# Norm weights on the rows of the output projections' weights, nine working tiles on 2 KB places, and the scores of two token tiles in one run

## The chip, the cores and the metric

The kernel runs on one core of a Trainium2 chip. Its engines work side by side, each through its own list of instructions in order: TensorE (PE) multiplies matrices into PSUM (eight banks of 128 partitions x 512 fp32 values), VectorE (DVE) and ScalarE (ACT) work on PSUM and SBUF, GpSimd (POOL) on SBUF only, and SyncE (SP) issues most of the transfers. An instruction that needs another engine's result waits for a semaphore, and everything behind it on its engine waits too. The metric is device time in microseconds, the median of several runs.

## The reference

Two layers of a trunk on a sequence of 512 tokens and a model width of 1024, all in fp32. Each layer normalises its input, projects it to 7,696 columns, runs four mixers on parts of these columns (retention, differential attention, a state-space mixer called SSD, and an mLSTM), each 512 wide, and adds the output projection of the four results:

```python
for l in range(DEPTH):
    u = rmsnorm(h, norm_w[l])
    ret_p, diff_p, ssd_p, ml_p = split_cols(u @ w_in[l], ...)
    ret_out  = retention_mixer(...) * silu(rz)
    diff_out = diff_attention_mixer(...) * silu(dz)   # _rms(out) * norm_w * (1.0 - lam_init)
    ssd_out  = _rms(y * silu(sz)) * ssd_norm_w[l]
    ml_out   = mlstm_mixer(...) * silu(mz)            # _layernorm(h) * norm_w
    mix = concatenate([ret_out, diff_out, ssd_out, ml_out])
    h = h + mix @ w_out[l]
return rmsnorm(h, final_norm_w)
```

Three of the mixers end in a norm with a weight for each of its columns; retention's has none. The differential attention has four heads with two sets of 64-wide queries and keys each: `s = q k` for both sets, a causal softmax of each, and `a = p0 - lam * p1` is multiplied with the values.

## The kernel before

**Tiles.** Tokens stand in four tiles of 128. The normalised input lies transposed in `uh` and `ul` (a rounded fp32r part and the rest), and each weight block of 128 x 512 is split the same way: `split_half` (L322) makes `whi` by a copy on ACT and `wlo` by a subtraction on DVE. A product is then three fp32r matmuls (hi-hi, lo-hi, hi-lo). `load_block` (L337) fetches a 512-column block of the input weights, `out_proj` (L552) the output weights of one mixer: four row blocks of 128 for each half of the 1024 columns, so eight split halves a mixer and layer.

**Order.** PE's order is written out by the program while it is built. `ORDER` (L48) lists the projections; they are the filler. The mixers are generators that the planner (`later`, `spawn`, `drive`, L120 to 147) interleaves with the filler: it adds up an estimated PE time (`clk`), and a mixer that yields a number is continued when that much estimated time has gone by. The numbers are in `W` (L55). `psum` (L169) hands out the eight PSUM banks, always the one that is planned to be free first; `free` gives a bank back with a `lag`, the estimated time until its readers are done. If the real readers are later, PE waits. The order of DVE, ACT, POOL and SP is chosen by the framework's scheduler, from the priorities of the instructions and its own costs (except in the start, where it is written out).

**The differential attention** (`diff`, L1031). For each head it splits the queries (`qs`), waits `dQ`, and then goes through the token tiles 0, 1, 2, 3. Tile t has (t+1) x 128 keys. Two banks take the scores of the two sets, by six matmuls of 64 rows each, two at a time on the two halves of the array (L1051). For each set DVE adds the mask on the diagonal block (L1055) and takes the negative maximum (L1056), ACT takes the exponential with its row sum (L1057); then DVE combines the two (L1061 to 1064). `diff_av` (L1071) comes `dT` + t x `dT1` later: it transposes `a` on PE, copies it out on ACT (odd tiles, L1078) or DVE (even tiles, L1080), and `dV` later multiplies it with the values into one bank for the head. Between the tiles lie waits of `dN` + t x `dN1` (1, 2, 3 and 4 in estimated us). `diff_fin` normalises the head and multiplies by `z` on POOL.

**Norm weights.** `ev_silu` (L459) evacuates the gate projections: tanh on ACT, `z` on DVE (L467). For `mz` and `dz` POOL then multiplies `z` by the row of the mixer's norm weights, broadcast over the partitions (L1154, L1158). For the SSD the weights come in at the end of `fin_s` (L936, on DVE). The broadcast rows lie in `rows`, 4,736 bytes a partition.

**The mLSTM** (`mlstm`, L744). For each token tile DVE builds a weight matrix by four instructions of 128 columns (L762), ACT takes its exponential (L764), DVE multiplies the scores by it (L769) and PE goes on with the result. POOL meanwhile scales queries (L758), and `fin_m` multiplies an earlier tile by `z` (L838).

**Places.** All tiles but the constants and `h` come from one pool. Working tiles `w` of 2 KB a partition are used in turn, seven of them; a score tile's two exponentials take one each.

## Time and profile before

| | us |
|---|---|
| median of 3 runs | 1041.19 |
| lowest and highest | 1039.27 and 1041.24 |
| profiled execution, its own time | 1043.25 |
| its span in the profile | 1041.2 |
| PE busy in the span | 1021.6 |
| DVE busy | 703.6 |
| ACT busy | 471.8 |
| POOL busy | 193.2 |

The span is the time between the first and the last instruction of the program; what lies around it (2.05 us in that execution) belongs to the execution's time. Matmuls are pipelined, so a busy PE is not necessarily a PE at its peak: the distance between the starts of two matmuls tells how fast it goes. Rows of the timeline hold start, duration, engine, line, operation, what is written and read, and how many instructions were merged; rows of groups hold the sum and the mean, and then the idle time before them and what ended it.

### The profile page before, as it was taken

Reading aid. Unit: us, or ns where it says so; the run is one execution under the profiler, and the core shown is the slowest. Engines: PE = TensorE matmul, PEld = TensorE weight load, DVE = VectorE, ACT = ScalarE, POOL = GpSimd, SP = SyncE. Lnnn points to the kernel's source line nnn. Section 1 sums busy time; section 2 is a strip of 40 time slices with the busy share of each in tenths; the row PEclk is TensorE's granted clock in tenths of the full one; section 3 lists DMA queues with packets and bytes.
Section 4 is the critical chain, followed back from the end, with each engine's and each line's share of the span. In section 5 each row is a group of like instructions: output and inputs, shape, how many; then the busy total and the mean of one; then the engine's idle time right before and its main releaser. Section 6 shows DMA issues by size and latency. Waiting matters only on the chain.

```text
span 1041.2 us, 14256 instructions
## 1 busy us (share of the span) xinstructions
PE 1021.6 (98%) x5116; PEld 834.7 (80%) x5116; DVE 703.6 (68%) x1501; ACT 471.8 (45%) x1050; POOL 193.2 (19%) x221
## 2 busy tenths in 40 slices
PE   7999999999999999999999999999999999999997
PEld 5788888877778888878887888787777888888786
DVE  5587686567777868546555967666577887773454
ACT  4444336644445444423353543575444553543322
POOL 3000143102111144022000013420021112520301
PEclk9999999999999999999999999999999999999999
DMA  7324322322212423323122432323132224233112
GB/s 296 108 73 120 102 71 82 101 82 82 60 42 88 132 64 101 115 71 126 42 82 82 129 94 72 91 81 102 62 97 65 82 82 122 82 95 108 49 54 82
DMA packets 39143, 95.54 MB, mean 92 GB/s; under 512 B 3592, under 2 KB 16520, under 8 KB 38944
## 3 DMA queue, kind: packets, MB, share of 16 engines
q1 hardware_dynamic: 38064, 93.18, 29.2%
q10 hardware_dynamic: 1008, 1.44, 0.4%
q8 instruction: 40, 0.66, 0.3%
q14 instruction: 31, 0.25, 0.1%
HBM read 92.47 MB, written 2.15 MB: 91 GB/s over the span
## 4 chain that ended last, share of the span: by engine, by line
PE 95%; DVE 3%; DMA 1%; ACT 1%; issue 0%; POOL 0%; SPq 0%; POOLq 0%; DVEq 0%; ACTq 0%
PE pspj L114 79%; PE psacc L114 6%; PE psS L114 6%; PE psS L118 4%; DVE wlo L329 1%; DMA cst<-in_consts_dram 1%; DVE w L762 1%; DVE z L467 0%; DVE s L1056 0%; ACT e L230 0%; ACT whi L327 0%; DVE e L305 0%; DVE z L1221 0%; DVE w L769 0%; DVE h L580 0%
## 5 line engine op out<-in xcount | busy, mean ns | idle before, releaser
L329 DVE TENSOR_TENSOR wlo<-raw,whi 128x512 fp32r<-128x512 f32 x298 | 212.0, 730 | 61.9 <-ACT whi L327 55.8
L327 ACT CAST whi<-raw 128x512 fp32r<-128x512 f32 x300 | 179.7, 619 | 129.4 <-PE pspj L114 77.4
L114 PE MATMUL pspj<-whi,uh 128*128 128x512 f32 x512 | 209.2, 409 | 0.9 <-DVE whi L327 0.6
L114 PE MATMUL pspj<-whi,ul 128*128 128x512 f32 x512 | 200.5, 392 | 0.0
L114 PE MATMUL pspj<-wlo,uh 128*128 128x512 f32 x512 | 199.9, 391 | 0.0
L114 PE MATMUL pspj<-uh,whi 128*128 128x512 f32 x448 | 179.1, 400 | 0.0
L114 PE MATMUL pspj<-uh,wlo 128*128 128x512 f32 x448 | 174.9, 390 | 0.0
L114 PE MATMUL pspj<-ul,whi 128*128 128x512 f32 x448 | 174.6, 390 | 0.0
L114 PEld LDWEIGHTS pspj<-whi,uh 128*128 128x128 f32 x512 | 96.6, 189 | 23.8 <-issue 3.0
L114 PEld LDWEIGHTS pspj<-wlo,uh 128*128 128x128 f32 x512 | 96.1, 188 | 21.0
L114 PEld LDWEIGHTS pspj<-whi,ul 128*128 128x128 f32 x512 | 96.8, 189 | 17.6 <-DVE ul L316 0.2
L114 PE MATMUL pspj<-whi,mh 128*128 128x512 f32 (+1 forms) x260 | 106.3, 409 | 3.6 <-DVE w L1080 3.6
L114 PE MATMUL pspj<-whi,ml 128*128 128x512 f32 (+1 forms) x260 | 103.1, 397 | 0.0
L114 PE MATMUL pspj<-wlo,mh 128*128 128x512 f32 (+1 forms) x260 | 102.9, 396 | 0.0
L114 PEld LDWEIGHTS pspj<-uh,wlo 128*128 128x128 f32 x448 | 84.1, 188 | 18.2
L114 PEld LDWEIGHTS pspj<-uh,whi 128*128 128x128 f32 x448 | 84.2, 188 | 17.3 <-issue 0.7
L114 PEld LDWEIGHTS pspj<-ul,whi 128*128 128x128 f32 x448 | 84.3, 188 | 15.9
L217 POOL TENSOR_TENSOR s<-s,nhalf 128x4 f32<-128x4 f32 (+1 forms) x44 | 36.1, 819 | 320.4 <-DVE s L1104 130.5
L509 DVE SCALAR_TENSOR_TENSOR e<-pspj,cvh,e 128x511 f32<-128x511 f32 (+2 forms) x90 | 66.9, 744 | 9.8 <-ACT e L507 8.7
L527 ACT ACTIVATE e<-pspj 32x512 f32<-32x512 f32 x96 | 56.6, 590 | 19.6 <-PE pspj L114 18.3
L580 DVE TENSOR_TENSOR h<-pspj,h 128x512 f32<-128x512 f32 (+1 forms) x65 | 43.6, 678 | 30.7 <-PE pspj L114 30.2
L114 PEld LDWEIGHTS pspj<-whi,mh 128*128 128x128 f32 x260 | 49.6, 191 | 15.3 <-DVE w L1080 4.4
(215 smaller groups left out, 1361.7 us busy)
## 6 DMA issues: line engine op xcount, KB each, us to landing
raw<-in_w_in_dram SPq DMA_DIRECT2D x118, 512.0 KB, 3.9
raw<-in_w_out_dram SPq DMA_DIRECT2D x32, 512.0 KB, 3.5
bcm<-adr SPq DMA_DIRECT2D x16, 256.0 KB, 3.4
bcm<-gdr SPq DMA_DIRECT2D x8, 256.0 KB, 3.4
out_dram<-z SPq DMA_DIRECT2D x7, 256.0 KB, 2.0
h<-in_x_dram SPq DMA_DIRECT2D x3, 512.0 KB, 8.4
rows<-in_rows_dram SPq DMA_DIRECT2D x2, 592.0 KB, 9.0
cst<-in_consts_dram SPq DMA_DIRECT2D x1, 1035.0 KB
```

What stands on the lines that cost most here:

```text
L114: self.nc.tensor.matmul(out, lhsT=lhsT, rhs=rhs, start=start, stop=stop, **kw)
L118: self.nc.tensor.transpose(out, src, self.ident if ident is None else ident)
L217: self.nc.gpsimd.tensor_tensor(out=out, in0=m, in1=self.nhalf[:, :n], op=ALU.pow)
L327: (nc.vector.tensor_copy if vector else nc.scalar.copy)(out=hi, in_=raw)
L329: eng.tensor_tensor(out=lo, in0=raw, in1=hi.bitcast(F32), op=ALU.subtract)
L509: nc.vector.scalar_tensor_tensor(acc[:, s:], p[:, 0:S - s], w[:, 3 - s:4 - s], acc[:, s:], ALU.mult, ALU.add)
L527: nc.scalar.activation(x[q * 32:q * 32 + 32, :], p[o * 32:o * 32 + 32, :], AF.Copy, scale=scale)
L580: nc.vector.tensor_tensor(out=hs, in0=p, in1=hs, op=ALU.add)
L762: nc.vector.scalar_tensor_tensor(w[:, h * P:(h + 1) * P], gb[:, h, :], self.al[:, t, h:h + 1], self.cap, ALU.add, ALU.min)
```

## The change

**Norm weights.** The weights of the three norms are no longer rows but columns: they stand behind the convolution parameters in `cv` (`V_M`, `V_S`, `V_D`), one column of 128 for each row block of the output weights. When `out_proj` splits the weights of these three mixers, each row is multiplied by its norm weight: ACT's copy becomes a scaled copy and DVE's subtraction a scaled subtraction. The POOL products at L1154 and L1158 are gone, and the end of `fin_s` becomes a scaled copy on ACT. Retention's weights are split as before. `rows` shrinks to 128 bytes a partition.

**Tiles and places.** Nine working tiles instead of seven (the lines that only say so are left out below, as is the removal of the two POOL products). The one pool becomes several: small tiles first, then `h` and the tiles of 2 KB and multiples of it, then the parameter columns, so that each large tile begins at a multiple of 2 KB.

**Scores.** For each head the token tiles go in two pairs, (2, 0) and (3, 1). The twelve score matmuls of a pair follow each other. Tile 0's scores lie in the last quarter of tile 2's banks; tiles 3 and 1 have two banks each. All banks of a pair are freed together with a lag of 4.0. Tiles 0 and 1 hold both exponentials in one working tile. `diff_av` of the first tile of a pair comes `dT` (now 9.0) later, that of the second another 3.0; the wait behind a pair is 5.0.

```diff
@@ -41,20 +41,28 @@
 GROUPS = {"r": 0, "d": 1, "s": 2, "m": 3}
-R_DNW, R_SNW, R_MNW, R_GB, R_AL, R_SD, R_LAM = 0, 128, 640, 1152, 1168, 1176, 1184
-R_W = 1184
+R_GB, R_AL, R_SD, R_LAM = 0, 16, 24, 32
+R_W = 32
+V_M, V_S, V_D, V_W = 80, 84, 88, 89
 ORDER = ["mv", "gates", "mq", "mk", "mlstm", "mo", "mz", "dk", "dq", "diff", "dv", "dz", "m", "xs", "bc", "ssd", "d",
          "rqk", "sz", "rv", "ret", "rz", "s", "r"]
+BIG = {"w", "e", "whi", "wlo", "uh", "ul", "bcm", "raw", "z", "ft", "mh", "ml", "qs"}
+END = {"cv", "cvh", "nlam", "aneg"}
 QS = 4
 W = {'norm': 9.0, 'g1': 1.5, 'g2': 7.3, 'g3': 1.8, 'g4': 12.4, 'mB': 1.8, 'mB3': 3.0, 'mC': 1.3, 'mN': 5.0, 'mF': 9.6, 'sB': 10.2,
-     'sN': 0.0, 'sF': 7.3, 'rC': 2.3, 'rN': 3.0, 'dT': 9.14, 'dN': 1.0, 'dM': 3.0, 'dV': 6.68, 'dF': 14.0,
-     'm0': 6.4, 's0': 8.8, 'dT1': 0.6, 'dN1': 1.0, 'hp': 100, 'he': 100, 'hr': 50, 'hd': 50, 'dS': 4.7, 'dQ': 6.0,
+     'sN': 0.0, 'sF': 7.3, 'rC': 2.3, 'rN': 3.0, 'dT': 9.0, 'dN': 5.0, 'dM': 3.0, 'dV': 6.68, 'dF': 14.0,
+     'm0': 6.4, 's0': 8.8, 'dT1': 3.0, 'hp': 100, 'he': 100, 'hr': 50, 'hd': 50, 'dS': 4.7, 'dQ': 6.0,
      'ha': 50}
...
@@ -96,7 +104,12 @@
         self.dbg = dbg or {}
         mk = lambda n, b, **k: ctx.enter_context(tc.tile_pool(name=n, bufs=b, **k))
         self.cp = mk("cp", 1)
+        self.small = mk("small", 1)
+        self.hp = mk("hp", 1)
         self.pool = mk("pool", 1)
+        self.end = mk("end", 1)
         self.ps = mk("ps", 1, space=bass.MemoryType.PSUM)
         self.banks = [(0.0, b) for b in range(8)]
         self.bank = {}
...
@@ -153,10 +166,11 @@
     def t(self, tag, shape, dt=F32, bufs=None):
         self.n += 1
-        return self.pool.tile(shape, dt, tag=tag, name=f"{tag}_{self.n}", bufs=bufs)
+        pool = self.pool if tag in BIG else self.end if tag in END else self.small
+        return pool.tile(shape, dt, tag=tag, name=f"{tag}_{self.n}", bufs=bufs)
     def pg(self):
-        return self.t("w", [P, 512], bufs=7)
+        return self.t("w", [P, 512], bufs=9)
     def ev(self):
         return self.t("e", [P, 512], bufs=4)
...
@@ -269,12 +283,14 @@
         nc = self.nc
         rows, lam, cv = self.prm
         self.cvh = self.t("cvh", [P, 2, 8, 5], bufs=2)
-        nc.vector.tensor_scalar(self.cvh, cv, 0.5, None, ALU.mult)
+        nc.vector.tensor_scalar(self.cvh, cv[:, 0:V_M].rearrange("p (a b c) -> p a b c", a=2, b=8), 0.5, None, ALU.mult)
         self.rw = lambda o, w: rows[:, o:o + w]
         lam_init = 0.8 - 0.6 * math.exp(-0.3 * l)
-        self.dnw = self.rw(R_DNW, P)
-        nc.vector.tensor_scalar(self.dnw, self.dnw, 0.5 * (1.0 - lam_init), None, ALU.mult)
-        lp = self.t("w", [P, 2, 64], bufs=7)
+        nc.vector.tensor_scalar(cv[:, V_D:V_W], cv[:, V_D:V_W], 0.5 * (1.0 - lam_init), None, ALU.mult)
+        self.nwc = {"m": [cv[:, V_M + k:V_M + k + 1] for k in range(4)],
+                    "s": [cv[:, V_S + k:V_S + k + 1] for k in range(4)],
+                    "d": [cv[:, V_D:V_W]] * 4, "r": [None] * 4}
+        lp = self.t("w", [P, 2, 64], bufs=9)
         ld = lam.rearrange("p (a b c) -> p a b c", a=2, b=2)
         nc.vector.tensor_tensor(out=lp, in0=ld[:, :, 0, :], in1=ld[:, :, 1, :], op=ALU.mult)
         ls = self.sm([P, 2])
...
@@ -319,24 +335,28 @@
                 yield 0
         self.done.add(("u", l, t))
-    def split_half(self, raw, j, vector=False):
+    def split_half(self, raw, j, vector=False, scale=None):
         nc = self.nc
         hi = self.t("whi", [P, 512], F32R, bufs=10)
         lo = self.t("wlo", [P, 512], F32R, bufs=10)
         with self.tc.high_priority(W["hp"]):
-            (nc.vector.tensor_copy if vector else nc.scalar.copy)(out=hi, in_=raw)
-            eng = nc.vector if j else nc.gpsimd
-            eng.tensor_tensor(out=lo, in0=raw, in1=hi.bitcast(F32), op=ALU.subtract)
+            if scale is not None:
+                nc.scalar.activation(hi, raw, AF.Copy, scale=scale)
+                nc.vector.scalar_tensor_tensor(lo, raw, scale, hi.bitcast(F32), ALU.mult, ALU.subtract)
+            else:
+                (nc.vector.tensor_copy if vector else nc.scalar.copy)(out=hi, in_=raw)
+                eng = nc.vector if j else nc.gpsimd
+                eng.tensor_tensor(out=lo, in0=raw, in1=hi.bitcast(F32), op=ALU.subtract)
         return hi, lo
-    def split_w(self, src, g):
+    def split_w(self, src, scales=(None, None)):
         raw = self.t("raw", [P, 2, 512], bufs=2)
         self.nc.sync.dma_start(out=raw, in_=src)
-        return [self.split_half(raw[:, j, :], 1) for j in range(2)]
+        return [self.split_half(raw[:, j, :], 1, scale=scales[j]) for j in range(2)]
     def load_block(self, name):
         b = BIDX[name]
-        return [q for g in range(4) for q in self.split_w(self.win[self.l, b, :, 2 * g:2 * g + 2, :], g)]
+        return [q for g in range(4) for q in self.split_w(self.win[self.l, b, :, 2 * g:2 * g + 2, :])]
     def start(self, evac):
...
@@ -552,7 +570,9 @@
     def out_proj(self, g, mixt, tok_outer=False, after=None, cut=False, heads=False):
         nc = self.nc
         gi = GROUPS[g]
-        w = [[x for q in range(2) for x in self.split_w(self.wout[self.l, gi, half, :, 2 * q:2 * q + 2, :], 2 * half + q)]
+        nw = self.nwc[g]
+        w = [[x for q in range(2) for x in self.split_w(self.wout[self.l, gi, half, :, 2 * q:2 * q + 2, :],
+                                                        nw[2 * q:2 * q + 2])]
              for half in range(2)]
         l = self.l
         order = [(t, hf) for t in range(NT) for hf in range(2)] if tok_outer else \
...
@@ -933,7 +953,7 @@
         self.rsqrt(f, m, 1)
         mix = self.pg()
         nc.vector.tensor_scalar(f, f, 0.5, None, ALU.mult)
-        nc.vector.scalar_tensor_tensor(mix, yd, f, self.rw(R_SNW, 512), ALU.mult, ALU.mult)
+        nc.scalar.activation(mix, yd, AF.Copy, scale=f)
         yield W["sF"]
         self.emit(l, t, "s", mix, res)
...
@@ -1038,33 +1058,44 @@
             o = self.psum("acc")
             r = self.sm([P, NT, 2], tag="rsum")
             ca = self.sm([P, NT])
-            for t in range(NT):
-                n = (t + 1) * P
-                ts_ = slice(t * P, n)
-                nm = self.sm([P, 2])
-                pe = [self.pg(), self.pg()]
-                sj = [self.psum("S"), self.psum("S")]
-                for i, (a, b) in enumerate(((0, 0), (0, 1), (1, 0))):
-                    for j, s in enumerate(sj):
-                        own = slice(j * 64, j * 64 + 64)
-                        self.mm(s[:, 0:n], lhsT=qp[a][own, ts_], rhs=k[h][b][own, 0:n], start=(i == 0), stop=(i == 2),
-                                share=0.5)
-                with self.tc.high_priority(W["hd"]):
-                    for j, s in enumerate(sj):
-                        nc.vector.tensor_tensor(out=s[:, ts_], in0=s[:, ts_], in1=self.mlow, op=ALU.add)
-                        nc.vector.tensor_reduce(out=nm[:, j:j + 1], in_=s[:, 0:n], axis=AX.X, op=ALU.max, negate=True)
-                        nc.scalar.activation(pe[j][:, 0:n], s[:, 0:n], AF.Exp, bias=nm[:, j:j + 1],
-                                             accum_out=r[:, t, j:j + 1])
-                        self.free(s, lag=2.5)
-                    rr = self.sm([P, 1])
-                    nc.vector.reciprocal(out=rr, in_=r[:, t, 1:2])
-                    nc.vector.scalar_tensor_tensor(ca[:, t:t + 1], rr, r[:, t, 0:1], self.nlam, ALU.mult, ALU.mult)
-                    a = pe[0]
-                    nc.vector.scalar_tensor_tensor(a[:, 0:n], pe[1][:, 0:n], ca[:, t:t + 1], pe[0][:, 0:n],
-                                                   ALU.mult, ALU.add)
-                self.spawn(self.diff_av(l, t, h, a, o, v), W["dT"] + t * W["dT1"])
-                yield W["dN"] + t * W["dN1"]
+            for tt in ((2, 0), (3, 1)):
+                bank = [self.psum("S"), self.psum("S")]
+                sj = {}
+                for i, t in enumerate(tt):
+                    n = (t + 1) * P
+                    if i and tt[0] == 2:
+                        sj[t] = [b[:, 3 * P:4 * P] for b in bank]
+                    else:
+                        if i:
+                            bank += [self.psum("S"), self.psum("S")]
+                        sj[t] = [b[:, 0:n] for b in bank[-2:]]
+                    new = not i or tt[0] == 3
+                    for m, (a, b) in enumerate(((0, 0), (0, 1), (1, 0))):
+                        for j, s in enumerate(sj[t]):
+                            own = slice(j * 64, j * 64 + 64)
+                            self.mm(s, lhsT=qp[a][own, t * P:n], rhs=k[h][b][own, 0:n], start=(new and m == 0),
+                                    stop=(m == 2), share=0.5, skip_group_check=True)
+                for i, t in enumerate(tt):
+                    n = (t + 1) * P
+                    nm = self.sm([P, 2])
+                    p0 = self.pg()
+                    pe = [p0[:, 0:n], p0[:, n:2 * n] if t < 2 else self.pg()[:, 0:n]]
+                    with self.tc.high_priority(W["hd"]):
+                        for j, s in enumerate(sj[t]):
+                            sd = s[:, t * P:n]
+                            nc.vector.tensor_tensor(out=sd, in0=sd, in1=self.mlow, op=ALU.add)
+                            nc.vector.tensor_reduce(out=nm[:, j:j + 1], in_=s, axis=AX.X, op=ALU.max, negate=True)
+                            nc.scalar.activation(pe[j], s, AF.Exp, bias=nm[:, j:j + 1], accum_out=r[:, t, j:j + 1])
+                        rr = self.sm([P, 1])
+                        nc.vector.reciprocal(out=rr, in_=r[:, t, 1:2])
+                        nc.vector.scalar_tensor_tensor(ca[:, t:t + 1], rr, r[:, t, 0:1], self.nlam, ALU.mult, ALU.mult)
+                        a = pe[0]
+                        nc.vector.scalar_tensor_tensor(a, pe[1], ca[:, t:t + 1], a, ALU.mult, ALU.add)
+                    self.spawn(self.diff_av(l, t, h, a, o, v), W["dT"] + i * W["dT1"])
+                self.free(*bank, lag=4.0)
+                yield W["dN"]
             self.spawn(self.diff_fin(h, o, r, zs, res, l))
             yield W["dM"]
...
@@ -1253,11 +1277,13 @@
     wo = i["w_out"].reshape(DEPTH, 4, 4, P, 2, 512)
     wo = np.ascontiguousarray(wo.transpose(0, 1, 4, 3, 2, 5))
     nrm = np.concatenate([i["norm_w"], i["final_norm_w"][None]], 0)
-    rows = np.concatenate([i["diff_norm_w"], i["ssd_norm_w"], i["mlstm_norm_w"], i["ssd_dt_bias"], i["mlstm_gate_b"],
-                           i["ssd_a_log"], i["ssd_d"], i["diff_lambda"].reshape(DEPTH, -1)], 1)
+    rows = np.concatenate([i["ssd_dt_bias"], i["mlstm_gate_b"], i["ssd_a_log"], i["ssd_d"],
+                           i["diff_lambda"].reshape(DEPTH, -1)], 1)
     cv = [np.concatenate([i[n + "_w"], i[n + "_b"][:, None]], 1).reshape(DEPTH, 5, 8, P)
           for n in ("ssd_conv", "mlstm_conv")]
-    cv = np.ascontiguousarray(np.stack(cv, 1).transpose(0, 4, 1, 3, 2))
+    cv = np.stack(cv, 1).transpose(0, 4, 1, 3, 2).reshape(DEPTH, P, -1)
+    cols = [i[n].reshape(DEPTH, -1, P).transpose(0, 2, 1) for n in ("mlstm_norm_w", "ssd_norm_w", "diff_norm_w")]
+    cv = np.ascontiguousarray(np.concatenate([cv] + cols, 2))
     return {"x": np.ascontiguousarray(i["x"][0]), "w_in": wb, "w_gate": wg, "w_out": wo,
             "norms": np.ascontiguousarray(nrm), "rows": np.ascontiguousarray(rows), "conv": cv, "consts": _consts()}
```

More of the change, by code (lines that the diff above doesn't have):

```diff
@@ L186, in setup @@
         nc = self.nc
-        self.h = [self.cp.tile([P, D], F32, name=f"h{t}") for t in range(NT)]
+        self.h = [self.hp.tile([P, D], F32, name=f"h{t}") for t in range(NT)]
         for half in range(2):
@@ L456, in proj_feat, with ev_silu @@
                 self.free(p, lag=3.0)
-    def ev_silu(self, dst, tag, bufs, nwt=None):
+    def ev_silu(self, dst, tag, bufs):
         nc = self.nc
@@ L467, in f @@
             nc.vector.scalar_tensor_tensor(z, th, 1.0, p, ALU.add, ALU.mult)
-            if nwt is not None:
-                nwt(z)
             dst.append(z)
@@ L606, in gates @@
             yield 0
-        gf = self.t("w", [32, 512], bufs=7)
+        gf = self.t("w", [32, 512], bufs=9)
         nc.scalar.copy(out=gf, in_=p[0:32, :])
@@ L665, in gates @@
         nc.vector.tensor_scalar(self.ncs, cs[:, :, 0:8], -1.0, None, ALU.mult)
-        st = self.t("w", [P, NT, 96], bufs=7)
+        st = self.t("w", [P, NT, 96], bufs=9)
         nc.gpsimd.memset(st, 0.0)
@@ L677, in gates @@
             self.tr(pr[0:96, t * P:(t + 1) * P], st[:, t, :])
-        arow = self.t("w", [8, 512], bufs=7)
+        arow = self.t("w", [8, 512], bufs=9)
         nc.scalar.copy(out=arow, in_=pr[0:8, :])
@@ L681, in gates @@
         nc.sync.dma_start(out=self.adr, in_=arow)
-        alr = self.t("w", [4, 512], bufs=7)
+        alr = self.t("w", [4, 512], bufs=9)
         nc.scalar.copy(out=alr, in_=pr[32:36, :])
@@ L686, in gates @@
         self.free(pr)
-        mr = self.t("w", [96, 512], bufs=7)
+        mr = self.t("w", [96, 512], bufs=9)
         nc.gpsimd.memset(mr, 0.0)
@@ L1151, in mixer @@
             return f
-        def times_mnw(z):
-            nc.gpsimd.tensor_tensor(out=z, in0=z, in1=self.rw(R_MNW, 512), op=ALU.mult)
-        def times_dnw(z):
-            z = z.rearrange("p (h d) -> p h d", h=4)
-            nc.gpsimd.tensor_tensor(out=z, in0=z, in1=self.dnw.unsqueeze(1).to_broadcast([P, 4, P]), op=ALU.mult)
         def got_q(h, x):
```

10 lines of the change are left out of this document (5 added, 5 removed).

## The prediction

> **What bounds the kernel now.** I read the head of the page first: the shares of the engines and the chain that ended last.
>
> ```profile
> span 1041.2 us, 14256 instructions
> PE 1021.6 (98%) x5116; PEld 834.7 (80%) x5116; DVE 703.6 (68%) x1501; ACT 471.8 (45%) x1050; POOL 193.2 (19%) x221
> PE 95%; DVE 3%; DMA 1%; ACT 1%; issue 0%; POOL 0%; SPq 0%; POOLq 0%; DVEq 0%; ACTq 0%
> ```
>
> TensorE (PE) is the bound nearly everywhere. Work taken off VectorE (DVE), ScalarE (ACT) or GpSimd (POOL) is worth something only where PE waits for it. So the second view is the list of PE's own waits (total, times, longest).
>
> ```profile
> PE pspj L114 <- DVE w L1080: 3.6, 2, 1.8
> PE psS L118 <- DMA cst<-in_consts_dram: 3.1, 1, 3.1
> PE psacc L114 <- DVE w L769: 2.6, 2, 1.3
> PE psS L118 <- DVE e L305: 1.6, 1, 1.6
> ```
>
> Two of the four are in the start (constants, the first norm), which the change leaves alone. The other two occur once in each of the two layers: L769 in the mLSTM, L1080 in the differential attention. They, and what PE itself does differently, are all that can move the end. Of the latter only the scores change.
>
> **Scores of two token tiles in one run.** The timeline of PE shows what a run of six score matmuls costs. I quote, for key widths 128, 256, 384 and 512, the projection matmul before the run, the run, and the second projection matmul behind it. The two rows of the chain below them give undisturbed streaming.
>
> ```profile
> 207.08 0.39 PE L114 MATMUL pspj<-wlo,uh 128*128 128x512 f32 x1
> 207.40 0.55 PE L114 MATMUL psS<-ft,qs 64*128 64x128 f32 x6
> ...
> 208.21 0.40 PE L114 MATMUL pspj<-whi,ul 128*128 128x512 f32 x1
> 209.14 0.39 PE L114 MATMUL pspj<-wlo,uh 128*128 128x512 f32 x1
> 209.46 0.63 PE L114 MATMUL psS<-ft,qs 64*128 64x256 f32 x6
> ...
> 210.35 0.39 PE L114 MATMUL pspj<-whi,ul 128*128 128x512 f32 x1
> 212.65 0.39 PE L114 MATMUL pspj<-wlo,uh 128*128 128x512 f32 x1
> 212.97 0.80 PE L114 MATMUL psS<-ft,qs 64*128 64x384 f32 x6
> ...
> 214.02 0.39 PE L114 MATMUL pspj<-whi,ul 128*128 128x512 f32 x1
> 217.00 0.39 PE L114 MATMUL pspj<-wlo,uh 128*128 128x512 f32 x1
> 217.32 0.96 PE L114 MATMUL psS<-ft,qs 64*128 64x512 f32 x6
> ...
> 218.55 0.39 PE L114 MATMUL pspj<-whi,ul 128*128 128x512 f32 x1
> 162.54 44.93 PE pspj L114 x198
> 503.25 16.04 PE pspj L114 x69
> ```
>
> A projection matmul takes 44.93/198 = 0.227 us. From start to start the four stretches last 1.13, 1.21, 1.37 and 1.55 us; each holds two projection matmuls (0.45). The score runs therefore cost 0.68, 0.76, 0.92 and 1.10 us. From 256 to 512 keys the cost grows by 0.34, so streaming 512 keys takes 0.68 and about 0.42 is fixed: the way in, the first and last pair of half-height matmuls, and the way out. It is paid 16 times a layer; the change pays it 8 times.
>
> 512+256 in one run: 1.10 + 0.34 = 1.44 instead of 1.86, saving 0.42. 384+128: 0.92 plus three short pairs, of 0.06 each by the slope or 0.17 each with the run's end in them, so 1.09 to 1.43 instead of 1.60, saving 0.17 to 0.51; I take 0.38. That makes 16 x 0.40 = **6.4 us**. No row shows 64-row matmuls that change tile in mid-run: if the pipeline empties between the two tiles, half the fixed cost stays (3.2); the upper end is 8 x (0.42 + 0.51) = 7.4. I take 6.4, since between pairs inside a run the weights change as well.
>
> **Norm weights on the weights' rows.** What goes and what comes:
>
> ```profile
> L1154 POOL TENSOR_TENSOR z<-z,rows 128x512 f32<-128x512 f32 x8 | 13.1, 1642 | 22.8 <-DVE z L467 22.8
> L1158 POOL TENSOR_TENSOR z<-z,rows 128x512 f32<-128x512 f32 x8 | 10.9, 1369 | 79.3 <-DVE z L467 79.3
> L936 DVE SCALAR_TENSOR_TENSOR w<-w,s,rows 128x512 f32<-128x512 f32 x8 | 6.0, 752 | 0.4
> L329 DVE TENSOR_TENSOR wlo<-raw,whi 128x512 fp32r<-128x512 f32 x298 | 212.0, 730 | 61.9 <-ACT whi L327 55.8 <-PE pspj L114 4.3 <-PE psS L118 0.9
> L465 ACT ACTIVATE e<-pspj 128x512 f32<-128x512 f32 x32 | 19.2, 599 | 50.1 <-PE pspj L114 49.8
> L507 ACT ACTIVATE e<-pspj,cvh 128x512 f32<-128x512 f32 x30 | 23.3, 777 | 17.1 <-PE pspj L114 17.1
> L118 PEld LDWEIGHTS psS<-cst,w 128*128 128x128 f32 x176 | 22.2, 142 | 6.2 <-DVE w L936 0.5 <-issue 0.4
> ```
>
> POOL loses 24 us. DVE loses 6.0 us at L936, and 48 weight halves (three groups, eight halves, two layers) turn from a subtraction into a scaled one. L936 is such a form, 752 ns against L329's 730: 0.02 more each, 1 us in all. ACT gains eight scaled copies (about 0.7 us each) and, per weight half, one column scalar: L507 has two and is 178 ns over L465, so 89 each, 48 x 0.089 = 4.3 us. All of this lies under PE; without that cover it would be ACT's 10 us against POOL's and DVE's gain. PE's waits name L327 and L329 nowhere behind the start, so the weights are split ahead of their use and 0.11 us more per half is hidden. One place has no cover: the transposes behind L936 waited 0.5 us in all. There an ACT copy now waits for the DVE scalar, with ACT's next casts and evacuations queued behind it, and PE waits for its transposes; standing behind such a cast itself it is 0 to 0.7 us late, once a layer: I take +0.5 in all. The shorter parameter row and the nine wider columns of the convolution parameters change two transfers that no row of PE's waits names: nothing.
>
> **The mLSTM's wait.** Where PE waits for L769, the timelines of DVE and POOL show:
>
> ```profile
> 104.15 0.34 DVE L762 SCALAR_TENSOR_TENSOR w<-bcm,g,cap 128x128 f32<-128x128 f32 x1
> 137.93 3.49 DVE L762 SCALAR_TENSOR_TENSOR w<-bcm,g,cap 128x128 f32<-128x128 f32 x4
> 142.21 0.68 DVE L769 SCALAR_TENSOR_TENSOR w<-psS,w 128x512 f32<-128x512 f32 x1
> 138.09 1.34 POOL L1154 TENSOR_TENSOR z<-z,rows 128x512 f32<-128x512 f32 x1 [3.46 <-DVE z L467]
> 139.51 1.29 POOL L838 TENSOR_TENSOR w<-w,z 128x512 f32<-128x512 f32 x1
> 140.76 2.25 POOL L758 TENSOR_TENSOR w<-w,ft 128x128 f32<-128x128 f32 x4
> ```
>
> Four L762 should take 4 x 0.34 = 1.4 us and take 3.5: while POOL runs L1154 and then L838, DVE gets one through each. Without L1154, L838 moves up to 138.1 and L758 to 139.4. DVE loses one block instead of two, but meets L758 sooner; I put L762's end 1.0 us earlier, so the 1.3 us wait shrinks to 0.3. Gain 2 x 1.0 = **1.9 us** (0 if another POOL instruction takes the slot, 2.6 if the wait goes).
>
> **The attention's wait.** L1080 empties a bank that the output projection wants next. Busy time by stretch (PE, PEld, DVE, ACT, POOL, then PE's granted clock), and the instructions concerned:
>
> ```profile
> 244.20:251.50 7.30, 5.65 (x28) 4.10 (x24) 7.16 (x19) 5.14 (x10) 3.16 (x3) 1.00 0.47 143
> 252.00:260.00 8.00, 8.00 (x34) 6.52 (x33) 4.90 (x7) 1.25 (x3) 2.58 (x4) 0.79 0.40 126
> ...
> 243.50 0.96 PE L114 MATMUL psS<-ft,qs 64*128 64x512 f32 x6
> 245.19 0.27 PE L118 MATMUL psS<-cst,w 128*128 128x128 f32 x1
> 251.29 0.28 DVE L1080 COPY w<-psS 128x128 f32<-128x128 f32 x1
> 251.10 0.69 ACT L1057 ACTIVATE w<-psS,s 128x512 f32<-128x512 f32 x1
> ```
>
> The transpose was there at 245.5; DVE, full for 7.2 of 7.3 us, came to it at 251.29. Behind it waits the whole PE queue, 1.8 us. Then the granted clock is 0.79 over 8 us: at half speed for 3.4 us, losing 1.7 more. Price 3.5 a layer, 7 in all.
>
> The Trainium skill ("TensorE: Matmul & The Clock Gate", "Why this matters for your kernels") asks for no PE idle gaps over about 3 us; by it a 1.8 us gap would cost 1.8 alone. The row shows 0.79 behind one, so the measurement decides; by the page the sum below would gain 3 us less.
>
> In the new order the second run (tiles 3 and 1) is planned 5 us behind the first, where tile 3 came behind waits of 1, 2 and 3 and three runs: some 2 to 3 us earlier. So two 512-wide maxima leave the crowded stretch, while tile 1's smaller ones move towards it. DVE gains little, but what PE asks for at 249 is then older. I take: two-thirds of the price goes, **4.5 us** (bounds: -2 if it grows, 7 if it goes). Nine instead of seven working tiles answer no wait in PE's list: nothing by themselves.
>
> **Sum.** 6.4 + 1.9 + 4.5 - 0.5 = 12.3 us. The profiled execution took 1041.2 in its span and 2.05 around it, 2.1 over the median of the runs; taken from that median (1041.2) it gives **1029 us**.
>
> **Rivals.**
>
> *The attention's wait stays or moves* (DVE's crowd is as dense as before, and the splits of the m weights are slightly dearer). For it: the same kinds of DVE work in the same place. Against: its bank's reader comes earlier. 6.4 + 1.9 - 0.5 saved: 1033.
>
> *Placement counts.* The new pools put every large tile on a multiple of 2 KB. Output projections stream at 16.04/69 = 0.232 us against 0.227; if that is their tiles' place, 756 such matmuls gain 0.005 each, 4 us, and with the whole attention wait gone 1022. Nothing else in the trace speaks for place.
>
> *Slower: banks run short.* The second run holds four of eight banks. With one or two accumulators and two projections open, the next transposes get one of these four, planned free after 4 us. But in the run of 243.50 the last exponential began at 251.10, 7.6 us on. It decides from the point where the exponentials are over some 5 us late; then PE waits 1 to 2 us per head and half the clock behind it. At 2.5 us in each of eight heads, 20 lost against 8.3 - 0.5 gained: 1053; in four heads 1043. Against it: in three of four heads of a layer DVE isn't full.
>
> The Trainium skill ("PSUM — Partial Sum Buffer", "Terms") says that two engines must not touch one bank at once, and here tile 0's scores lie in tile 2's bank; no run here shows the wait that this makes, and by it the chain would be a few tenths later.
>
> *No difference:* the pipeline empties between tiles (3.2 left) and new waits of 3 us eat it: 1040.
>
> **Chances.** Forecast 0.44, wait stays 0.20, placement 0.11, banks 0.17, no difference 0.08. About 0.2% (2 us) is what a measurement can tell from none: faster 0.75, within it 0.09, slower 0.16. Range 1019 to 1043; it leaves out the better half of the placement case and most of the bank case. The forecast's own range is 1024 to 1033.
>
> **What would show it.** Right: 8 score runs of 12 a layer, each stretch of 512+256 near 1.9 us from start to start; no L1154 beside L762 and PE's wait for L769 under 0.5; PE's wait near 250 us under 1 and the granted clock 1.00 behind it. Wrong: PE waiting for an exponential (L1057's successor) or its bank before transposes, clock below 1.00 elsewhere in 205 to 320 us, or projection matmuls off 0.227.

## The result, and the profile after

The changed kernel takes 1055.35 us (median of 6 runs, 1049.9 to 1056.46) beside 1040.34 (1038.71 to 1041.77) for the kernel before on the same chip: 1.0124 times as long, 95% interval 1.0107 to 1.014. It is 15 us slower, where 1029 and a gain of 12 were forecast. Below, every kernel is given by its difference from the kernel before in the same series, since that one's median moves by about 1 us from series to series.

The head of the page of the changed kernel:

```profile
span 1054.7 us, 14219 instructions
PE 1021.2 (97%) x5116; PEld 842.9 (80%) x5116; DVE 692.6 (66%) x1493; ACT 482.2 (46%) x1058; POOL 167.2 (16%) x205
PE 88%; DVE 6%; ACT 2%; issue 1%; DMA 1%; POOL 1%; SPq 0%; POOLq 0%; ACTq 0%; DVEq 0%
```

The work of the other engines changed in the way that was planned (POOL 26 us less, ACT 10 us more, DVE 11 us less, where the forecast's terms give 5). But PE's share of the chain that ended last fell from 95% to 88%: PE waits more. Its own waits (what was waited for, then total, times, longest):

```profile
PE pspj L127 <- ACT w L1090: 6.8, 2, 3.4
PE psS L131 <- DVE ml L566: 4.7, 2, 2.3
...
PE pspj L127 <- DVE h L600: 3.0, 2, 1.5
PE psacc L127 <- DVE w L897: 2.8, 2, 1.5
PE pspj L127 <- DVE z L487: 2.1, 2, 1.0
...
PE psacc L127 <- DVE w L789: 0.7, 2, 0.3
```

The first three rows and that of `z` were not there before: 16.6 us, each wait once a layer, all between 240 and 303 us in the first. The wait for L897 (the masks of the state-space mixer, SSD) is new too. The attention's old wait (L1080 before, L1111 now) is gone, and the mLSTM's (L769, now L789) went from 2.6 to 0.7.

The largest wait in the timelines of PE and ACT:

```profile
298.49 0.39 PE L127 MATMUL pspj<-uh,wlo 128*128 128x512 f32 x1
302.29 0.79 PE L127 MATMUL pspj<-uh,whi 128*128 128x512 f32 x1 [3.41 <-ACT w L1090]
...
301.67 0.47 ACT L1090 ACTIVATE w<-psS,s 128x256 f32<-128x256 f32 x1 [0.55 <-DVE s L1089]
```

A projection wants a bank, and gets one of the four that the run of tiles 3 and 1 took at 294.6. PE stands until the exponential of tile 1 has read it. And busy time by stretch (PE, PEld, DVE, ACT, POOL, then the granted clock), behind three such waits and the SSD's:

```profile
264.00:274.00 10.00, 6.16 (x36) 4.44 (x35) 8.87 (x27) 5.13 (x20) 2.71 (x5) 0.98 0.35 105
273.50:277.50 4.00, 4.00 (x13) 3.23 (x14) 1.66 (x5) 0.00 (x0) 0.00 (x0) 0.57 0.00 0
...
302.00:307.50 5.50, 5.21 (x14) 4.14 (x15) 3.80 (x10) 1.43 (x5) 0.00 (x0) 0.50 0.00 0
410.00:420.00 10.00, 8.51 (x33) 7.06 (x32) 7.00 (x16) 3.75 (x8) 1.83 (x2) 0.68 0.37 107
```

Half the clock behind the 3.4 us wait, behind the 2.3 us wait, and behind the SSD's 1.5; not behind the 1.5 us wait for `h` at 266. The Trainium skill ("TensorE: Matmul & The Clock Gate", "Why this matters for your kernels") asks for no PE idle gaps over about 3 us; here gaps of 1.5 and 2.3 us were followed by it as well.

The score runs did what was forecast:

```profile
207.23 0.39 PE L127 MATMUL pspj<-wlo,uh 128*128 128x512 f32 x1
207.55 1.07 PE L127 MATMUL psS<-ft,qs 64*128 64x384 f32 x12
...
208.89 0.39 PE L127 MATMUL pspj<-whi,ul 128*128 128x512 f32 x1
...
213.90 0.39 PE L127 MATMUL pspj<-wlo,uh 128*128 128x512 f32 x1
214.22 1.32 PE L127 MATMUL psS<-ft,qs 64*128 64x512 f32 x12
...
215.81 0.40 PE L127 MATMUL pspj<-whi,ul 128*128 128x512 f32 x1
```

From start to start 1.66 and 1.91 us; less two projection matmuls (0.45) the runs cost 1.21 and 1.46, where the separate ones cost 0.68 + 0.92 = 1.60 and 1.10 + 0.76 = 1.86. Each join saves 0.39 to 0.40, 16 of them 6.3 us.

### The profile page after: what moved, and what is told of

It is laid out like the page before. It is cut to its first block, busy times and chain, and to the rows that moved or that the text cites. A ratio compares the mean times of both kernels' runs of the same rounds, so it can differ in the third digit from the quotient of the medians.

```text
span 1054.7 us, 14219 instructions
## 1 busy us (share of the span) xinstructions
PE 1021.2 (97%) x5116; PEld 842.9 (80%) x5116; DVE 692.6 (66%) x1493; ACT 482.2 (46%) x1058; POOL 167.2 (16%) x205
## 4 chain that ended last, share of the span: by engine, by line
PE 88%; DVE 6%; ACT 2%; issue 1%; DMA 1%; POOL 1%; SPq 0%; POOLq 0%; ACTq 0%; DVEq 0%
PE pspj L127 74%; PE psacc L127 5%; PE psS L127 4%; PE psS L131 4%; DVE wlo L349 1%; DMA raw<-in_w_in_dram 1%; DVE h L600 1%; DVE w L893 1%; DMA cst<-in_consts_dram 1%; POOL s L231 1%; ACT e L244 0%; ACT e L1129 0%; ACT w L1090 0%; DVE ft L549 0%; DVE z L1245 0%
## 5 line engine op out<-in xcount | busy, mean ns | idle before, releaser
L349 DVE TENSOR_TENSOR wlo<-raw,whi 128x512 fp32r<-128x512 f32 x250 | 176.4, 724 | 66.1 <-ACT whi L347 60.8
L347 ACT CAST whi<-raw 128x512 fp32r<-128x512 f32 x252 | 150.4, 619 | 111.5 <-PE pspj L127 66.8
```

What stands on the lines that cost most here:

```text
L347: (nc.vector.tensor_copy if vector else nc.scalar.copy)(out=hi, in_=raw)
L349: eng.tensor_tensor(out=lo, in0=raw, in1=hi.bitcast(F32), op=ALU.subtract)
```

## The experiments

Two theories stood after the traces. **A, banks run short** (the prediction's slower rival): the run of tiles 3 and 1 keeps four of eight banks longer than planned. **B**: something in the move of the norm weights, the nine tiles or the places makes PE wait. In the diffs, "..." marks what is left out, and the lines of planning numbers are cut to the numbers that change.

### Which part costs the time

The pairing alone, on the kernel before:

```diff
--- the kernel before
-            for t in range(NT):
+            for tt in ((2, 0), (3, 1)):
...
-      'dT': 9.14, 'dN': 1.0, 'dT1': 0.6, 'dN1': 1.0,
+      'dT': 9.0, 'dN': 5.0, 'dT1': 3.0,
```

> The kernel before with only the scores paired (tiles 2 and 0, then 3 and 1, and the three planning values that go with it); norm weights, tiles and places as before. Theory A (banks run short: the run of tiles 3 and 1 keeps four of the eight banks until its last exponential, and what is loaded next into one of them waits with the whole PE queue behind): the waits of the kernel after for the exponential, for h, z and the masks come back here, 240 to 320 us and again 760 to 835 us, at least 6 us of them with the half clock behind; time 1045 to 1055. Theory B (the norm weights' move or the places make the kernel late, the pairing gains its 6.4 us): 1032 to 1036, and no PE wait above 1 us in 205 to 320 us but the old one of 1.8.

Measured: 1052.37 us, 11.5 slower than before, 1.0116 (1.0098 to 1.0134). PE's waits:

```profile
PE pspj L114 <- ACT w L1070: 6.8, 2, 3.4
PE psS L118 <- DVE ml L548: 4.7, 2, 2.3
...
PE pspj L114 <- DVE h L580: 3.0, 2, 1.5
...
PE pspj L114 <- DVE z L467: 2.1, 2, 1.0
```

The same four waits to the tenth. The pairing alone makes them; the norm weights, tiles and places have no part in them. The wait for the SSD's masks, which theory A had named with them, is not here. Nor is half the clock in its place: in this profiled execution the clock stays full behind the same waits of the first layer, 1.00 over 273.5 to 277.5 us behind that of 2.3 us and over the next row behind that of 3.4 us. The second layer's 3.4 us, at 812, is followed by 0.53 over 812.2 to 818.0.

```profile
300.50:306.00 5.50, 5.50 (x26) 4.50 (x27) 3.74 (x10) 1.79 (x4) 0.00 (x0) 1.00 0.00 0
```

The other half, the kernel after without the pairing:

```diff
--- the kernel after
-            for tt in ((2, 0), (3, 1)):
+            for t in range(NT):
...
-      'dT': 9.0, 'dN': 5.0, 'dT1': 3.0,
+      'dT': 9.14, 'dN': 1.0, 'dT1': 0.6, 'dN1': 1.0,
```

> The kernel after with the scores of each tile in a run of their own and the old planning values; norm weights on the rows of the weights, nine working tiles and the 2 KB places stay. Theory A (banks): no new waits in the attention; what stays are the mLSTM wait cut to 0.7 (1.9 gained), output projections at 0.227 (about 3.5 gained), perhaps the attention's wait of 3.5 a layer as before, so 1030 to 1036. Theory B: the new waits in 205 to 320 us and in the state-space mixer at 411 us are here, time 1050 to 1060.

Measured: 1044.36 us, 3.5 slower than before, 1.0029 (1.0014 to 1.0044). Neither theory had this: no bank waits, as A said, but no gain either.

```profile
PE pspj L127 <- DVE w L1100: 4.3, 2, 2.2
...
PE psacc L127 <- DVE w L897: 3.2, 2, 1.6
```

The attention's old wait stays (L1100), the mLSTM's is cut (0.7), and the SSD's wait for L897 is here: it belongs to this half of the change. So there are two causes, and each needs its own experiments.

### Cause one: the banks

Only tiles 2 and 0 in one run; tiles 3 and 1 in runs of their own, two banks each. A head's total spacing stays at 10 planned us:

```diff
--- the kernel after
-            for tt in ((2, 0), (3, 1)):
+            for tt, lag, gap in (((2, 0), 4.0, 4.0), ((3,), 2.5, 4.0), ((1,), 2.5, 2.0)):
...
-                self.free(*bank, lag=4.0)
-                yield W["dN"]
+                self.free(*bank, lag=lag)
+                yield gap
```

> The kernel after, but only tiles 2 and 0 share a run (in two banks); tile 3 and tile 1 each have a run and two banks of their own, planned 4 us apart, so that never four banks are held by one run. Theory A (banks): the gain of four of the eight joins a layer stays (3.2 us), the new waits go, 1027 to 1036, and PE waits for no exponential for longer than 1 us. Theory B (the rest of the change): 1048 to 1058.

Measured: 1035.59 us, 5.3 faster than before, 0.9951 (0.9932 to 0.9969). The four bank waits are gone, but for 0.5 us a layer at `z`; the attention's old wait is gone too. The SSD's stays. That is A's forecast, near its upper end.

Is there a bank for PE, and the plan only picks the wrong one? One number, so that the four banks count as free 8 us after their run, about when they are:

```diff
--- the kernel after
-                self.free(*bank, lag=4.0)
+                self.free(*bank, lag=4.0 if tt[0] == 2 else 8.0)
```

> The kernel after with one number changed: the four banks of the run of tiles 3 and 1 are planned free 8 us after it instead of 4, near to when the last exponential really reads them, so that the planner takes other banks first. If the waits come from a wrong time in the plan (banks are there, the plan takes the wrong ones): PE's waits for the exponential, h, z and the masks shrink below 1 us each, time 1040 to 1046. If there are not enough banks (theory A as it was predicted): the planner still has to take banks that are not free, the waits stay above 5 us in all, 1050 to 1058.

Measured: 1057.09 us, 15.9 slower than before, 1.0156 (1.011 to 1.0202).

```profile
PE pspj L127 <- DVE s L1092: 9.1, 2, 4.5
PE psS L131 <- DVE ml L566: 4.6, 2, 2.3
...
```

No better than the kernel after (15.0): a truthful lag doesn't help, there is no other bank to take. The plan's own clock says the same. In the kernel before, and with two banks a run, no bank is asked for ahead of its planned time; in the kernel after it happens ten times, 0.4 to 1.4 us ahead, and with the longer lag ten times again.

More room in time instead: 7 planned us behind each run instead of 5.

```diff
--- the kernel after
-      'dN': 5.0,
+      'dN': 7.0,
```

> The kernel after with one number changed: 7 us of planned time behind a run of paired scores instead of 5, so that the four banks of the run of tiles 3 and 1 are out of use before the next run asks for its own. Theory A (four banks held for 7.6 us by a plan that gives them 4, with the next run 5 us on): the waits for the exponential, h, z and the masks go or fall below 1 us each, while all eight joins a layer stay, 1033 to 1040. Rival E (the crowd of VectorE work sets the waits, whatever the spacing): they only move, 1046 to 1058.

Measured: 1069.48 us, 28 slower than before, 1.0263 (1.0238 to 1.0287). Both theories missed.

```profile
PE psS L127 <- DVE ft L532: 12.4, 2, 6.2
PE psS L131 <- DVE w L1111: 6.7, 6, 1.7
PE pspj L127 <- DVE w L1111: 6.2, 2, 3.1
```

The waits for the exponential, `h`, `ml` and `z` are gone, as A said. But the attention is now 4 planned us longer in each of four heads and slides into the start of the SSD, where PE waits 6.2 us at 344 for a feature (L532), and for the copies of the attention's transposes (L1111). Two of the three rows are again waits for banks, those of the transposes: the 3.1 us before a projection at 256 stand where the old wait of the attention stood. So this run says that room in time takes the four new waits away, and that there is no such room; it doesn't price the banks.

The last of this group asks whether four banks at once are too many even when they are given back one pair after the other, or whether it is the lump of two tiles' work on DVE. It is the kernel with seven tiles from the next part (1028.89 us), with tile 1's scores again directly behind tile 3's:

```diff
--- the kernel with two banks a run and seven tiles
-            for tt, lag, gap in (((2, 0), 4.0, 4.0), ((3,), 2.5, 4.0), ((1,), 2.5, 2.0)):
+            for tt in ((2, 0), (3, 1)):
...
+                    if tt[0] == 3:
+                        self.free(*bank[2 * i:2 * i + 2], lag=2.5)
+                        yield 2.0 if i else 4.0
```

> The kernel with two banks a run and seven tiles (1028.9 us), but tile 1's scores again directly behind tile 3's in one run of TensorE, in banks of their own (four in use), while the masks, maxima and exponentials of tile 1 are planned 4 us behind those of tile 3 and each tile's two banks are given back by themselves. Theory A (four banks at once are too many, also when they are given back one pair after the other): waits of 1 us and more come back in 230 to 300 us, the 3.2 us of the second join are eaten: 1029 to 1037. Rival F (the lump of two tiles' work on VectorE is the cause, not the number of banks): no new wait above 1 us, 1024 to 1027.

Measured: 1039.5 us, 1.6 from before, 0.999 (0.9976 to 1.0005), so 10.8 more than the kernel that it was made from, where the joins alone would have saved 3.2.

```profile
PE pspj L127 <- ACT w L1090: 6.9, 2, 3.5
...
```

The exponential's wait is back in full, at 3.5 us, and the plan asks for a bank ahead of its time again, four times. So four banks in one run are too many also when they are given back pair by pair; the time lies above A's range. But the run doesn't part number from lump. DVE's order is the scheduler's, and it kept the lump: in the last head of the first layer, whose scores run at 289.04, DVE had done the masks of both tiles by 293.05, before the first maximum, and the first and the last exponential are close together:

```profile
294.66 0.69 ACT L1090 ACTIVATE w<-psS,s 128x512 f32<-128x512 f32 x1 [1.37 <-DVE s L1089]
...
297.42 0.47 ACT L1090 ACTIVATE w<-psS,s 128x256 f32<-128x256 f32 x1 [0.20 <-DVE s L1089]
```

Whether four banks would do with readers further apart stays open. What is excluded is that DVE has too much work in all. The whole stretch of the attention, first in the kernel after, then in the one with two banks and seven tiles:

```profile
205.00:330.00 125.00, 116.72 (x607) 94.64 (x606) 82.25 (x208) 57.48 (x157) 9.67 (x16) 0.96 0.23 72
```

```profile
205.00:330.00 125.00, 124.49 (x653) 100.60 (x652) 91.17 (x222) 62.78 (x165) 11.47 (x20) 1.00 0.23 72
```

With two banks DVE does 9 us more work in the same 125 us, and PE doesn't wait for it.

### Cause two: nine working tiles

The SSD's wait comes with the norm weights' half of the change, though it touches neither PE's order nor DVE's masks. The timelines of POOL and DVE show it. In the kernel before, POOL's skip product (L890, now L910) waits for a working tile until PE has read one, and runs behind the masks:

```profile
406.71 1.33 POOL L890 TENSOR_TENSOR w<-w,rows 128x512 f32<-128x512 f32 x1 [4.11 <-PE psacc L114]
```

The clearest pair is the kernel without pairs, with seven tiles (an experiment below) and with nine, since PE comes to the product that has to wait at the same time in both, 403.3. Seven masks of the token tile before it, the skip product of that tile, and what follows; first with seven tiles:

```profile
378.10 3.74 DVE L893 SCALAR_TENSOR_TENSOR w<-bcm,g,cap 128x128 f32<-128x128 f32 x7
391.24 1.50 POOL L910 TENSOR_TENSOR w<-w,rows 128x512 f32<-128x512 f32 x1
...
394.77 0.68 DVE L549 TENSOR_TENSOR ft<-ft,e 128x512 f32<-128x512 f32 x1
394.80 1.56 POOL L884 TENSOR_TENSOR w<-w,g 128x512 f32<-128x512 f32 x1 [2.06 <-ACT w L881]
```

Then with nine:

```profile
378.12 4.52 DVE L893 SCALAR_TENSOR_TENSOR w<-bcm,g,cap 128x128 f32<-128x128 f32 x7
380.61 1.09 POOL L910 TENSOR_TENSOR w<-w,rows 128x512 f32<-128x512 f32 x1
...
395.70 1.05 POOL L884 TENSOR_TENSOR w<-w,g 128x512 f32<-128x512 f32 x1 [3.54 <-ACT w L881]
...
395.73 1.56 DVE L549 TENSOR_TENSOR ft<-ft,e 128x512 f32<-128x512 f32 x1
```

With nine tiles the skip product runs 10 us earlier, beside DVE's masks, and the seven masks take 4.52 us instead of 3.74. DVE stays 0.8 to 1.0 us late from there on. So POOL's L884, which writes a working tile too, now comes 0.03 us ahead of L549 instead of 0.03 behind, and it is DVE that is held up (1.56 us instead of 0.68) and not POOL. That makes 1.85 us, of which PE waits 1.6. The waiting tile's own masks add nothing: its skip product, at 399.29, slows two of them (2.12 us instead of 1.45), but POOL's L548 then meets fewer of the other six, and all eight take 4.22 us with nine tiles and 4.14 with seven. The Trainium skill ("SBUF — State Buffer", "Who interferes with whom") says that a DVE instruction with two inputs in SBUF contends with a GpSimd instruction that reads SBUF; these rows agree.

Seven tiles again, under two banks a run, in the kernel without pairs, and in the kernel after (nine lines each, all alike):

```diff
-        return self.t("w", [P, 512], bufs=9)
+        return self.t("w", [P, 512], bufs=7)
```

> The kernel with only tiles 2 and 0 in one run and two banks a run (1035.6 us), with seven working tiles of 2 KB again instead of nine. Theory C (the ninth tile lets GpSimd start the state-space mixer's skip product, w<-w,rows, some 7 us earlier, beside VectorE's masks, which get slower by it; so PE waits 1.5 us for a mask product at 401 us and again in layer 2): that wait goes, with the half clock that may follow it, 1029 to 1033. Rival D (the wait comes from somewhere else, for instance from output projections that stream faster and reach it sooner): the wait stays at 1.3 to 1.6, 1035 to 1037, or new waits for working tiles come, 1036 to 1042.

> The kernel after without the pairing (1044.4 us), with seven working tiles instead of nine: norm weights on the rows of the weights and 2 KB places alone. Theory C (the nine tiles make the state-space wait): 1038 to 1040, that is 4 to 6 us less. Rival D: 1043 to 1046, the wait of 1.6 us for the mask product stays.

> The kernel after with seven working tiles instead of nine and nothing else: theory C adds up with theory A: the state-space wait goes (5 to 6 us less), the banks' waits of 8 us a layer stay: 1047 to 1051. If the two have one cause, either both go (below 1040) or nothing changes (1053 to 1057).

Measured, with the difference from the kernel before beside that of the same kernel with nine tiles:

| | us | seven tiles | nine tiles | ratio to before |
|---|---|---|---|---|
| two banks a run | 1028.89 | -12.4 | -5.3 | 0.988 (0.986 to 0.9899) |
| without pairs | 1038.51 | -2.7 | +3.5 | 0.9971 (0.9957 to 0.9986) |
| kernel after | 1046.53 | +5.5 | +15.0 | 1.0056 (1.0039 to 1.0072) |

The row for L897 is gone from PE's waits in all three. Theory C holds each time; two of the times lie 0.1 and 0.5 us below its range. The sizes (7.1, 6.2 and 9.5 us) are larger than the two waits of 1.5. Most of the rest goes with the clock: in the runs of two banks with nine tiles the mean granted clock was 0.991 to 0.995, with seven 0.993 to 0.997. Not every 1.5 us is followed by half the clock, which may also be why these kernels scatter more; the rest isn't accounted for row by row.

The skip product by itself, nine tiles kept and only this product written later:

```diff
--- the kernel with two banks a run
-            yd = self.pg()
-            nc.gpsimd.tensor_tensor(out=v8(yd), in0=v8(xt), in1=b8(self.rw(R_SD, 8)), op=ALU.mult)
             yield W["sB"]
+            yd = self.pg()
+            nc.gpsimd.tensor_tensor(out=v8(yd), in0=v8(xt), in1=b8(self.rw(R_SD, 8)), op=ALU.mult)
```

> The kernel with two banks a run and nine working tiles (1035.6 us), with the skip product of the state-space mixer (GpSimd's w<-w,rows) written behind the planned pause for the masks instead of ahead of it, so that it can't run beside VectorE's masks however many working tiles are free. If GpSimd's instruction beside VectorE's is what made PE wait 1.5 us for the mask product: that wait falls below 0.5, 1028 to 1031, with nine tiles. If the nine tiles make the wait in another way (the masks' own tiles, the order of VectorE): it stays, 1034 to 1037. The skip product then comes later and may itself be waited for: VectorE's sum behind it by some tenths.

Measured: 1031.75 us, 8.3 faster than before, 0.9917 (0.9901 to 0.9934), where the kernel that it was made from was 5.3 faster and the one with seven tiles 12.4.

```profile
PE psacc L127 <- DVE w L897: 1.5, 2, 0.9
...
377.07 1.09 POOL L911 TENSOR_TENSOR w<-w,rows 128x512 f32<-128x512 f32 x1
```

The wait falls from 1.5 to 0.9 and 0.6, not below 0.5, and 3.0 of the 7.1 us come back. The edit moved the skip product (here L911) of the waiting tile away from its masks, which take 3.84 us instead of 4.20. That of the tile before still runs beside them, at 377.07; those seven masks take 4.52 us as above, and L884 again holds up L549 (1.56 us). So the skip product is part of the wait, and by the rows these two are what is left; neither was moved by itself.

### The place of the tiles

In the changed kernel the output projections stream faster. The last 69 matmuls of them in the chain of layer 1:

```profile
513.26 15.69 PE pspj L127 x69
```

15.69/69 = 0.2274 us, where it was 0.2325. Does a multiple of 2 KB do this? All large tiles and `h` 128 bytes on, in the kernel without pairs:

```diff
--- the kernel without pairs
         self.hp = mk("hp", 1)
+        self.shift = self.hp.tile([P, 32], F32, name="shift")
```

> As the kernel after without the pairing (norm weights on rows of weights, nine working tiles), but every large tile and the residual stream 128 bytes further on, so that none lies on a multiple of 256 bytes, where in the kernel before only the output projections' left operand did not. If such places cost (output projections took 0.232 us a matmul there, 0.227 in the kernel after): all 512-wide matmuls of the projections at 0.231 to 0.233, 4400 of them by 0.005, about 20 us over the kernel without the pairing. If the place is nothing and the 0.227 comes from elsewhere: the same time as that kernel within 2 us, and output projections at 0.227.

Measured: 1043.69 us, 2.8 slower than before, 1.002 (1.0006 to 1.0035), as without the shift (3.5). The chain:

```profile
504.75 15.68 PE pspj L128 x69
```

0.2272: the absolute place is nothing. Then only the left operands of the output projections (`mh`, `ml`), in a pool of their own, 128 bytes on, with all else in place:

```diff
--- the kernel with two banks a run
+        self.sp = mk("sp", 1)
+        self.shift = self.sp.tile([P, 32], F32, name="shift")
+        self.mp = mk("mp", 1)
...
-        pool = self.pool if tag in BIG else self.end if tag in END else self.small
+        pool = self.mp if tag in {"mh", "ml"} else self.pool if tag in BIG else self.end if tag in END else self.small
```

> The kernel with two banks a run and nine tiles (1035.6 us), with the left operands of the output projections alone moved 128 bytes on (offset 128 in 2 KB), all other large tiles at 0. Theory G (it is the place of one operand against the other that counts: in the kernel before these tiles lay at 640 and the weights at 768, 128 apart in 256): the output projections of the m, s and r groups take 0.232 us a matmul again, about 2 to 3.5 us in all. Rival H (what made 0.227 is something else, the pools' order or the engines' writes): 0.227 to 0.228 stays.

Measured: 1036.01 us in one run, which the time can't tell from the kernel that it was made from (1032.87 to 1038.04). The streaming can:

```profile
499.75 16.09 PE pspj L130 x69
```

16.09/69 = 0.2332. What counts is the place of one operand against the other: 128 bytes apart in 256 costs 0.005 to 0.006 us a matmul in these rows, for the 756 such matmuls an estimated 3 to 4 us.

## Why the prediction was wrong

Two steps failed, both in what the sum put at nothing. The price of four banks in one run stood in a rival and not in the sum: the scores' part of the change was to gain 6.4 + 4.5 us and lost 8.2 (with seven tiles) to 11.5. And the nine working tiles, "nothing by themselves", cost 6.2 to 9.5. The steps in their order:

- **Joined runs, 6.4 us**: right. 6.3 by the rows above; PE's pipeline doesn't empty between the tiles, and the stretch of 512+256 has the 1.9 us that was named.
- **Norm weights**: right. The scaled copies and subtractions (ACT's plain copy in the third row):

```profile
L344 ACT ACTIVATE whi<-raw,cv 128x512 fp32r<-128x512 f32 x48 | 33.4, 718 | 26.8 <-PE pspj L127 14.0 <-DMA raw<-in_w_out_dram 12.7
L345 DVE SCALAR_TENSOR_TENSOR wlo<-raw,cv,whi 128x512 fp32r<-128x512 f32 x48 | 35.6, 756 | 9.8 <-ACT whi L344 9.5
L347 ACT CAST whi<-raw 128x512 fp32r<-128x512 f32 x252 | 150.4, 619 | 111.5 <-PE pspj L127 66.8 <-DMA raw<-in_w_in_dram 35.6 <-DMA raw<-in_w_out_dram 2.5
```

  99 ns more on ACT for a half (89 were taken) and 26 on DVE against 730 (20 taken), hidden as said. The 0.5 us for the copy at the end of `fin_s` did not show in the kernel after: no row of PE's waits there names L956 (0.4 us, once, in the kernel with the later skip product).
- **The mLSTM's wait, 1.9 us**: right, in size and reason (2.6 to 0.7). L1154 is gone from POOL, L858 stands in its place (139.27), and the four L782 take 2.60 us instead of 3.49:

```profile
139.04 2.60 DVE L782 SCALAR_TENSOR_TENSOR w<-bcm,g,cap 128x128 f32<-128x128 f32 x4
```

- **The attention's wait, 4.5 us**: the old wait goes altogether in the kernels with the new order, more than was taken; only with the wider gap does it stand, at 3.1 us a layer. The half clock in its price is no fixed amount: it followed some waits of this size and not others, and not the old wait itself in the kernel without pairs (2.2 us, then 1.00 over 251 to 260). (By the 1.8 us alone the term would have been some 2 us smaller, not 3.) But the step asked only whether that one wait goes or moves; what came into its place was left to the rival.
- **"Nine instead of seven working tiles answer no wait in PE's list: nothing by themselves"**: this step failed, by 6.2 to 9.5 us. The reasoning looked for a wait on PE that more tiles would end. But the tiles held POOL back, not PE, and that was of use: it kept the skip product out of the masks' way. POOL's row with "4.11 <-PE psacc" stood in the trace before and wasn't asked for.
- **The chance of the banks, 0.17**: the step that decided. The mechanism was written down much as it then happened: four of eight banks, planned free after 4 us, read later. Its sign of being wrong, PE waiting for an exponential, came. Only the longest wait is for one of the four banks, by a projection; the other three are for banks from which DVE still has to make `h`, `ml` and `z`, while those four are out. The last head's run of tiles 3 and 1, its last exponential, and the busy time between:

```profile
294.61 1.31 PE L127 MATMUL psS<-ft,qs 64*128 64x512 f32 x12
...
302.66 0.47 ACT L1090 ACTIVATE w<-psS,s 128x256 f32<-128x256 f32 x1 [0.42 <-DVE s L1089]
...
295.90:303.20 7.30, 3.89 (x16) 2.94 (x15) 5.56 (x14) 3.22 (x9) 2.60 (x5) 0.84 0.00 0
```

  The run ends at 295.92, the exponential at 303.13, 7.2 us later, though DVE is busy for only 5.56 of 7.30 us; in the four heads of the layer it is 6.1 to 8.0 us. The rival was set to decide from some 5 us. So "against it: in three of four heads of a layer DVE isn't full" was the wrong ground: the exponentials are late in a head where DVE isn't full, too. And the lateness alone isn't it: with two banks a run it is still about 5 us, and no bank is missing. The price: new waits of 16.6 us, less the old wait of 4.2 and the joins' 6.3, is 6.1, with half the clock behind some of them; measured between the kernels with seven tiles, with and without pairs, 8.2 us. That the rival's time, 1053, is near the 1055 measured is luck: with seven tiles it is 1046.5, and the other 9 us are the tiles'.
- **The few tenths for tile 0's scores in tile 2's bank** stood on no row. In the first head of the kernel after, DVE's first mask in that bank starts at 208.66, when the whole run is over (208.62); no row of PE's waits shows it.
- **Placement** was a rival with 0.11, because "nothing else in the trace speaks for place". The streaming came as it said (0.232 to 0.227, 3 to 4 us by the estimate above). Its reason, multiples of 2 KB, was wrong.

Step by step, by kernels: norm weights and places -2.7 (the profiled spans: 1036.4 against 1041.2), then nine tiles +6.2, then pairing +11.5. That these make the measured +15.0 proves nothing, since each is measured on top of the one before; in another order the parts are others (pairing +8.2 before the nine tiles, the tiles then +9.5), so they add up only roughly. The kernel with two banks a run and seven tiles is faster than both, 1028.89 us; that this is the time forecast is chance, since it has half of the joins and a term, the place, that the forecast left out.

## What to carry to other kernels

Before work is put into longer runs, count the buffers that a run holds until its last reader, and compare the plan's release with the trace's last read; a saving of 0.4 us a join is worth nothing if one bank comes late. The Trainium skill ("Perfetto Trace Analysis", "Optimization Strategy") names too little PSUM as one reason for gaps that repeat on the engine that should be busy; here they repeated in both layers, to the tenth.

An additional buffer is not without effect just because nobody on the critical engine waits for one: look at the idle time of every engine for waits that a buffer ends, and ask what the freed instruction will run beside.

Change one resource at a time: three parts of one change had effects of -2.7, +6.2 and +11.5 in this order, and the best kernel keeps one of them and half of another.

## What was not expected of the hardware

- A matmul of 512 columns streamed at 0.227 us where both operands lay alike within 256 bytes, and at 0.232 to 0.233 where they lay 128 bytes apart (640 and 768 within 2 KB in the kernel before; 128 and 0 in the experiment). A shift of both changed nothing. Only these places were tried.
- Half the granted clock followed PE gaps of 1.5 us (at 413 us), 2.3 and 3.4 us in the kernel after, and didn't follow another of 1.5 us (at 268). With the pairing alone it didn't follow the same gaps of 2.3 and 3.4 us in the first layer (1.00 behind both), and followed that of 3.4 us in the second (0.53). In these runs the length of a gap doesn't decide it.
